# A three-block network in split fp32 on one core: the wide products of a block in a row, tiles 32 bytes further on, and another end of the convolution

## The chip, the cores and the metric

The program runs on one core of a Trainium2 chip. The metric is the device time of one execution in microseconds (us); smaller is better. What is given of the kernel before is the median of three runs, and the profile of one more execution.

## The reference

Three blocks of two layers work one after the other on `x` of 256 tokens by 1024 features in fp32. Almost all the work is dense products with weights that are each used once. The parts that matter here, cut:

```python
def swiglu_ffn(x, w_in, w_out):
    gate, up = jnp.split(x @ w_in, 2, axis=-1)
    return (jax.nn.silu(gate) * up) @ w_out

def conformer_conv_module(x, w_in, b_in, w_dw, b_dw, ln_g, ln_b, w_out, b_out):
    a, gate = jnp.split(x @ w_in + b_in, 2, axis=-1)
    h = a * jax.nn.sigmoid(gate)
    h = lax.conv_general_dilated(h, w_dw[:, None, :], ..., feature_group_count=D_MODEL) + b_dw
    h = jax.nn.silu(layer_norm(h, ln_g, ln_b))
    return h @ w_out + b_out

def reference(x, ...):
    x = first_block(x, ...)     # ffn, conv, ffn; ffn, hgrn, ffn
    x = second_block(x, ...)    # ffn, dsa attention, ffn; ffn, diff attention, ffn
    return third_block(x, ...)  # pool, mlp; moba attention, mlp
```

A feed-forward layer ("ffn") has 22 groups of 128 hidden features; the two of the third block ("mlp") have 4096 hidden features and a squared relu. The convolution is causal, 31 taps wide, one filter for each feature.

## The kernel before

**Split products.** Each fp32 operand of a big product is held as a rounded part and the rest, both in a format (`F32R`) that TensorE multiplies in one pass: weights as `hi` and `lo` (ScalarE rounds at L330, VectorE subtracts at L334), activations as `xh`, one tile that holds for each of 8 blocks of features first the rounded part of the 256 tokens and then the rest. A product of both is made of three: rounded by rounded, rounded by rest, rest by rounded. Weights come through in 413 chunks of 1 MB.

**Three forms of product.** `proj_pair` (L603 to L605) keeps an activation part of 128 tokens in the array (stationary) and streams 512 columns of weights (moving). `downs` (L644) does the same for the second product of a layer, with the hidden activations as the stationary operand: `hh` and `hl` in the feed-forward layers, `oscT` and `ov` in hgrn, `xh` itself in the other mixers. `wide_products` is turned round: it keeps 128 columns of weights in the array and streams activations. For each of the 8 blocks of features it issues a **wide** product (L565: `hi` against 512 columns, that is both parts of `xh`) and a **narrow** one (L566: `lo` against the 256 columns of the rounded part), and both add into one accumulator tile, `ps` or `tr`. Such a set of 8 wide and 8 narrow products is called a block here. Wide and narrow alternate, but for the last pair, which is the other way round.

**Layers.** A feed-forward layer begins with `first` (four weight chunks by `proj_pair`), goes on with pairs of blocks (one in `ps`, one in `tr`) and 24 or 48 products of `downs` behind each second pair, and ends in `finish`, which does `downs` for four held chunks, first for tokens 0 to 127 (accumulators `a0`, `a1`), then for the others (`a2`, `a3`). Under the second half it normalizes the first, and its transposes for the next layer (L502) are issued ten products before the end.

**The convolution.** Features stand on partitions, in 8 blocks of 128. Blocks 3 to 7 are convolved on TensorE (L930, fp32): ScalarE copies the gated block into two phases, `ph` (L928, four copies for a block), then 16 taps are multiplied for each half of the block, and ScalarE brings each half back with its bias (L934, two copies for a half). Then layer norm: VectorE subtracts a mean (L951), TensorE sums squares (L959) and the last block's mean (`rest`, L961), a reciprocal root goes over VectorE and GpSimd, TensorE spreads it over the partitions (`rb`, L973), and for two blocks at a time VectorE subtracts and multiplies (L978, L979), ScalarE applies silu and rounds (L983, L985), VectorE takes the rest (L986). The accumulators of the output projection begin with a product that puts the bias in (L990). In `ps`, `a0` to `a3` and `tr` are the PSUM tiles' names, with one buffer for each `a` and two for `ps` and `tr`: `var` is in `a3` and `ps`, `rest` in `a0`, `rb` in `a1`.

**What sets the order.** The code is recorded through a tile framework whose scheduler sets the order on each engine by the tiles' dependences, with a few fixed points (`issue`). Tiles lie in pools, one behind the other in each partition of SBUF, every tile rounded up to 32 bytes. `raw`, `hi`, `lo` and `xh` come first; then the pool of small tiles, `tiny`, with the 4-byte tile `prime`; then the pools that each layer opens and closes. In the built program `hi`, `lo` and `xh` begin 32 bytes behind a multiple of 64 (`xh` at byte 136416), and the layers' pools begin at byte 174784, a multiple of 64; `hh`, `hl`, `mh`, `ml`, `oscT` and `ov`, which lie in them, begin at multiples of 64. (`mh` and `ml` are the split memory tokens of the third block.)

The lines that the prediction speaks of, by operation: L330 and L334 splits; L502, L711 transposes; L552 to L554 `proj_u`, a run of narrow products (256 columns) in conv and hgrn; L1076 the conversion of hgrn's masks from 32 bits to 8.

Of the kernel before, what the change touches and what calls it, by code (L numbers as in the profile page):

```python
# [11 lines left out]
F32 = mybir.dt.float32  # L12
# [4 lines left out]
AF = mybir.ActivationFunctionType  # L17
OP = mybir.AluOpType
# [3 lines left out]
S = 256  # L22
# [270 lines left out]
class _K:  # L293
# [137 lines left out]
    def prime(self, func, after):  # L431

        n = after.shape[0]
        t = self.tiny.tile([128, 1], F32, name="prime", bufs=1)
        self.nc.scalar.activation(t[:n], after, func, scale=0.0)

    def square(self, src, st, n):
# [118 lines left out]
    def wide_products(self, w, p):  # L556


        wh, wl = w
        mm = self.nc.tensor.matmul  # L560
        for b, o in enumerate(p):
            for k in range(8):
                c = slice(256 * k + 128 * b, 256 * k + 128 * b + 128)
                x = self.both[:, k]
                hi = lambda start, stop: mm(o, lhsT=wh[:, c], rhs=x.rearrange("p i t -> p (i t)"), start=start, stop=stop)  # L565
                lo = lambda: mm(o[:, :256], lhsT=wl[:, c], rhs=x[:, 0], start=False, stop=False)  # L566
                if k < 7:
                    yield hi(k == 0, False)
                    yield lo()
                else:  # L570
                    yield lo()
                    yield hi(False, True)

    def added(self, out, p, n=slice(0, 128)):
        self.nc.scalar.activation(out, p[n, 256:], AF.Copy)  # L575
# [293 lines left out]
    def conv(self, act):  # L869
        nc, tc = self.nc, self.tc  # L870
        with tc.tile_pool(name="cv", bufs=2) as cp:
# [4 lines left out]
            y = cp.tile([128, 8, S], F32, name="y", bufs=1)  # L876
# [6 lines left out]
            brow = self.tmp.tile([128, D], F32, name="xn", bufs=1)  # L883
            i = _ROW[("conv_b_out", (0,))]
# [5 lines left out]
            ones = cp.tile([128, 128], F32R, name="ones", bufs=1)  # L890
            nc.scalar.activation(ones, pick[:, :128], AF.Copy)
            bias = cp.tile([128, D], F32R, name="bias", bufs=1)
            nc.scalar.activation(bias, brow, AF.Copy)
            nc.vector.tensor_tensor(bias[32:33], brow[32:33], bias[32:33].bitcast(F32), op=OP.subtract)
            self.rows_ahead("conv")

            mean = self.ps("a2")
# [6 lines left out]
            def summed(j):  # L904
                nc.tensor.matmul(mean[:, :S], lhsT=means[:, 1], rhs=y[:, j], start=(j == DVE_BLOCKS), stop=(j == DVE_BLOCKS - 1))
# [11 lines left out]
            for j in range(DVE_BLOCKS, 8):  # L917
                p = self.turned(p4[j]) if j < 4 else self.proj_u(self.take(("U", "conv", j)), act)
                g = cp.tile([128, S], F32, name="gl")
                sg = gated(j, p, g)  # L920
                x = ph[j % 2]
                pc = self.ps(f"a{j % 2}").rearrange("p (g t) -> p g t", g=4)
                for i in range(2):
                    w = cp.tile([128, 16, 128], F32, name="taps", bufs=3)
                    nc.sync.dma_start(w.rearrange("p d c -> p (d c)"), self.a["ctaps"][2 * (j - DVE_BLOCKS) + i])
                    gv = g[64 * i:64 * i + 64].rearrange("p (t a) -> p a t", a=2)
                    for a in range(2):
                        nc.scalar.activation(x[64 * a:64 * a + 64, i, 15:], gv[:, a], AF.Copy)  # L928
                    for d in range(16):
                        nc.tensor.matmul(pc[:, i], lhsT=w[:, d], rhs=x[:, i, d:d + S // 2], start=(d == 0), stop=(d == 15))  # L930
                    yv = y[64 * i:64 * i + 64, j].rearrange("p (t a) -> p a t", a=2)
                    for a in range(2):
                        h = slice(64 * a, 64 * a + 64)
                        nc.scalar.activation(yv[:, a], pc[h, i], AF.Identity, bias=self.col("bph", 2 * j + i)[h])  # L934
                if j < 7:
                    summed(j)
                self.split_ahead(2)
                n = self.TAPS_BEHIND[j - DVE_BLOCKS]
                for at in left[:n]:
                    tap(*at)  # L940
                    if at[1] == CW - 1:
                        summed(at[0])
                left = left[n:]
            self.prime(AF.Silu, sg[:, :1])

            var = [self.ps("a3"), self.ps()]
            rest = self.ps("a0")
            for b in ((0, 1), (2, 3), (4, 5), (6,), (7,)):
                n = len(b)
                yb = y[:, b[0]:b[0] + n]  # L950
# [1 line left out]
                sq = cp.tile([128, 2, S], F32, name="sq")  # L952
# [4 lines left out]
                for i in range(n):  # L957
                    for m in range(2):
                        nc.tensor.matmul(var[m][:, :1], lhsT=sq[:, i, 128 * m:128 * m + 128], rhs=means[:, 0, :1],  # L959
                                         start=(b[i] == 0), stop=(b[i] == 7))  # L960
            nc.tensor.matmul(rest[:, :S], lhsT=means[:, 0], rhs=y[:, 7], start=True, stop=True)  # L961
            t = lambda nm: self.tiny.tile([128, 2], F32, name=nm, bufs=1)
# [4 lines left out]
            nc.gpsimd.tensor_tensor(r, v, self.mhalf[:, :2], op=OP.pow)  # L967

            dg = cp.tile([128, 2, 128], F32, name="sg")
            rb = self.ps("a1")  # L970
            for m in range(2):
                nc.vector.tensor_scalar(dg[:, m], self.ident, r[:, m:m + 1], float(D), op0=OP.mult, op1=OP.mult)
                nc.tensor.matmul(rb[:, 128 * m:128 * m + 128], lhsT=means[:, 0], rhs=dg[:, m], start=True, stop=True)  # L973
            oact = self.new_act()
            for g in range(4):
                yg = y[:, 2 * g:2 * g + 2]
                for b in range(2):
                    nc.vector.tensor_tensor(yg[:, b], yg[:, b], rest[:, :S], op=OP.subtract)  # L978
                nc.vector.tensor_tensor(yg, yg, rb[:, None, :S].to_broadcast([128, 2, S]), op=OP.mult)  # L979
                z = cp.tile([128, 2, S], F32, name="sq")  # L980
                for b in range(2):
                    j = 2 * g + b
                    nc.scalar.activation(z[:, b], yg[:, b], AF.Silu, bias=self.col("lnb", j), scale=self.col("lng", j))  # L983
                h = oact[0][:, 2 * g:2 * g + 2]
                nc.scalar.activation(h, z, AF.Copy)  # L985
                nc.vector.tensor_tensor(oact[1][:, 2 * g:2 * g + 2], z, h.bitcast(F32), op=OP.subtract)  # L986
            acc = self.new_acc()
            for m in range(2):
                for n in range(2):
# [5 lines left out]
    def hgrn(self, act):  # L995
        nc, tc = self.nc, self.tc
        with tc.tile_pool(name="hg", bufs=2) as ho, ExitStack() as es:
            hp = es.enter_context(tc.tile_pool(name="hgi", bufs=2))
            masks = hp.tile([128, 7, 64], U8, name="masks", bufs=1)
# [73 lines left out]
            p4 = self.first("hgrn", _U_ORDER["hgrn"][:2], act)  # L1073
            mi = self.tmp.tile([128, D], I32, name="xn", bufs=1)
            nc.sync.dma_start(mi[:, :448], self.a["k_masks"])
            nc.vector.tensor_copy(masks.rearrange("p l t -> p (l t)"), mi[:, :448])  # L1076
            self.rows_ahead("hgrn")
            for j in range(4):
                pf, pq = ([self.turned(p4[2 * j + i]) for i in range(2)] if j < 2 else
                          [self.proj_u(self.take(("U", "hgrn", 2 * j + i)), act) for i in range(2)])  # L1080
                vals = elems(j, pf, pq)
                for lev in range(8):
                    scores(j, *vals, lev)
            for n, s in enumerate(self.HALVES):
# [8 lines left out]
            for m in range(2):  # L1093
                for h in range(8):
                    o = oacc[m][h // 4][:, 128 * (h % 4):128 * (h % 4) + 128]
# [15 lines left out]
            oact = [ho.tile([128, 8, 256], F32R, name="o" + t, tag=t, bufs=1) for t in ("v", "scT")]  # L1111
# [750 lines left out]
```

## Time and profile before

| what | value |
|---|---|
| median of three runs | 2610.27 us (2608.87 to 2611.88) |
| the profiled execution | 2617.61 us, of which its span from first to last instruction is 2615.1 us |
| TensorE | 2570.5 us busy, 98% of the span, 13302 products |
| VectorE, ScalarE | 1953.7 us (75%), 1504.6 us (58%) |
| TensorE's granted clock | 0.995 of full speed, as a mean |

"Busy" is the union of the recorded durations. TensorE's products overlap, so its busy time does not say how fast they follow each other; for that one reads the distance from one start to the next in the timeline. The profiled execution took 7.3 us longer than the median of the others.

### The profile page before, as it was taken

How to read it: one execution, taken by the hardware profiler on the slowest of the kernel's cores; microseconds unless marked ns; L12 is line 12 of the kernel's file. 1: busy time of each engine (PE TensorE's matmuls, PEld its weight loads, DVE VectorE, ACT ScalarE, POOL GpSimd, SP SyncE). 2: the span in 40 equal slices, each digit the busy share in tenths (PEclk: the TensorE clock that was granted, in tenths of full speed). 3: DMA queues.
4: the chain of work that ended last, by engine and by line, in shares of the span. 5: the costliest groups of instructions: out<-in, count | busy, mean ns of one | idle time of the engine just before them, and what ended most of it. 6: DMA issues, size and time to landing. Idle time of an engine off the chain costs nothing.

```text
span 2615.1 us, 37057 instructions
## 1 busy us (share of the span) xinstructions
PE 2570.5 (98%) x13302; PEld 2153.1 (82%) x13302; DVE 1953.7 (75%) x4175; ACT 1504.6 (58%) x3373; POOL 72.4 (3%) x158
## 2 busy tenths in 40 slices
PE   8999999999999999999999999999999999999999
PEld 7888888888888888888778888877788788877887
DVE  7868587687668886886969779777866866677664
ACT  5655455555644555655765565575655655566553
POOL 0000000000000000000000000000100000000000
PEclk9999899999999999999999999999999999999999
DMA  8847376486424675684448668653555545542552
GB/s 326 304 164 282 145 274 233 159 333 228 176 82 178 256 291 188 259 330 181 177 153 324 241 235 330 232 212 129 209 187 184 188 161 199 187 171 97 193 182 92
DMA packets 92711, 554.14 MB, mean 212 GB/s; under 512 B 10716, under 2 KB 11756, under 8 KB 38384
## 3 DMA queue, kind: packets, MB, share of 16 engines
q1 hardware_dynamic: 92528, 551.79, 57.3%
q8 instruction: 104, 1.70, 0.3%
q14 instruction: 79, 0.65, 0.1%
HBM read 550.62 MB, written 1.13 MB: 211 GB/s over the span
## 4 chain that ended last, share of the span: by engine, by line
PE 57%; issue 35%; ACT 3%; DVE 3%; DMA 1%; POOL 1%; SPq 0%; POOLq 0%; ACTq 0%; DVEq 0%
PE a L644 20%; PE ps L565 8%; PE tr L565 8%; PE ps L566 4%; PE tr L566 4%; PE a L603 2%; PE a L604 2%; PE a L605 2%; PE a L930 2%; DVE lo L334 1%; ACT hi L330 1%; PE tr L502 1%; DMA raw<-in_wall 1%; ACT junk L440 1%; POOL ry L446 1%
## 5 line engine op out<-in xcount | busy, mean ns | idle before, releaser
L334 DVE TENSOR_TENSOR lo<-raw,hi 128x512 fp32r<-128x512 f32 x1652 | 1062.5, 683 | 157.9 <-ACT hi L330 154.1
L330 ACT ACTIVATE hi<-raw 128x512 fp32r<-128x512 f32 x1652 | 926.9, 622 | 319.9 <-PE a L644 156.6
L565 PE MATMUL ps<-xh,hi 128*128 128x512 f32 x1344 | 489.1, 398 | 1.2 <-DVE sg L576 1.2
L565 PE MATMUL tr<-xh,hi 128*128 128x512 f32 x1312 | 477.5, 398 | 1.2 <-DVE ml L511 1.2
L566 PE MATMUL ps<-xh,lo 128*128 128x256 f32 x1344 | 349.9, 281 | 0.3 <-DVE lo L334 0.3
L566 PE MATMUL tr<-xh,lo 128*128 128x256 f32 x1312 | 341.9, 281 | 0.0
L644 PE MATMUL a<-hi,hh 128*128 128x512 f32 x960 | 309.5, 396 | 0.0
L644 PE MATMUL a<-hi,hl 128*128 128x512 f32 x960 | 309.3, 396 | 0.0
L644 PE MATMUL a<-lo,hh 128*128 128x512 f32 x960 | 308.9, 395 | 0.0
L565 PEld LDWEIGHTS ps<-xh,hi 128*128 128x128 f32 x1344 | 252.7, 188 | 51.3 <-DVE sg L576 1.9
L565 PEld LDWEIGHTS tr<-xh,hi 128*128 128x128 f32 x1312 | 247.7, 189 | 45.2 <-DVE ml L511 1.5
L566 PEld LDWEIGHTS ps<-xh,lo 128*128 128x128 f32 x1344 | 253.9, 189 | 15.9 <-DVE lo L334 0.5
L566 PEld LDWEIGHTS tr<-xh,lo 128*128 128x128 f32 x1312 | 248.1, 189 | 15.0
L644 PEld LDWEIGHTS a<-hi,hl 128*128 128x128 f32 x960 | 180.1, 188 | 43.4
L644 PEld LDWEIGHTS a<-lo,hh 128*128 128x128 f32 x960 | 180.1, 188 | 43.0
L644 PEld LDWEIGHTS a<-hi,hh 128*128 128x128 f32 x960 | 179.8, 188 | 40.1 <-ACT sg L832 0.2
L603 PE MATMUL a<-hi,xh 128*128 128x512 f32 x512 | 202.2, 396 | 3.1 <-ACT xh L510 1.9
L605 PE MATMUL a<-hi,xh 128*128 128x512 f32 x512 | 201.7, 395 | 0.0
L604 PE MATMUL a<-lo,xh 128*128 128x512 f32 x512 | 200.5, 392 | 0.2 <-DVE lo L334 0.2
L1186 DVE SCALAR_TENSOR_TENSOR adaj<-adaw,cond 128x1024 bf16<-128x1024 f32 x144 | 175.3, 1217 | 17.3 <-DMA adaw<-in_ada 17.0
L576 DVE TENSOR_TENSOR h<-h,tr 128x256 f32<-128x256 f32 x140 | 58.6, 419 | 150.7 <-ACT h L575 149.9
L575 ACT ACTIVATE h<-tr 128x256 f32<-128x256 f32 x140 | 53.6, 383 | 156.7 <-PE tr L565 156.6
(380 smaller groups left out, 3310.4 us busy)
## 6 DMA issues: line engine op xcount, KB each, us to landing
raw<-in_wall SPq DMA_DIRECT2D x413, 1024.0 KB, 4.8
adaw<-in_ada SPq DMA_DIRECT2D x144, 512.0 KB, 6.6
taps<-in_ctaps SPq DMA_DIRECT2D x10, 1024.0 KB, 7.4
G<-in_rows SPq DMA_DIRECT2D x16, 512.0 KB, 4.4
pg<-in_rows SPq DMA_DIRECT2D x12, 512.0 KB, 4.8
xn<-modd SPq DMA_DIRECT2D x12, 512.0 KB, 5.3
cond<-condd SPq DMA_DIRECT2D x7, 512.0 KB, 5.2
memt<-in_mem SPq DMA_DIRECT2D x4, 512.0 KB, 3.3
```

Source lines behind the costliest of these rows:

```text
L330: self.nc.scalar.activation(h[:, c], r[:, c], AF.Copy)
L334: self.nc.vector.tensor_tensor(l[:, c], r[:, c], h[:, c].bitcast(F32), op=OP.subtract)
L565: hi = lambda start, stop: mm(o, lhsT=wh[:, c], rhs=x.rearrange("p i t -> p (i t)"), start=start, stop=stop)
L566: lo = lambda: mm(o[:, :256], lhsT=wl[:, c], rhs=x[:, 0], start=False, stop=False)
L575: self.nc.scalar.activation(out, p[n, 256:], AF.Copy)
L576: self.nc.vector.tensor_tensor(out, out, p[n, :256], op=OP.add)
L603: yield self.nc.tensor.matmul(p, lhsT=xh[:, k, t], rhs=wh[:, c], start=(k == 0), stop=False)
L604: yield self.nc.tensor.matmul(p, lhsT=xh[:, k, t], rhs=wl[:, c], start=False, stop=False)
L605: yield self.nc.tensor.matmul(p, lhsT=xl[:, k, t], rhs=wh[:, c], start=False, stop=(k == 7))
L644: mm = lambda l, r, i, st, sp: nc.tensor.matmul(acc[i], lhsT=l[:k, t], rhs=r[:k, 1024 * b + 512 * i:1024 * b + 512 * i + 512], start=st, s ...
L930: nc.tensor.matmul(pc[:, i], lhsT=w[:, d], rhs=x[:, i, d:d + S // 2], start=(d == 0), stop=(d == 15))
L1186: self.nc.vector.scalar_tensor_tensor(junk, self.ada_w.pop(n), 1.0, self.cond, op0=OP.mult, op1=OP.mult, accum_out=self.mods[k][:, c:c + 1])
```

## The change

It has six parts. (1) `prime` takes 64 bytes in place of 4, of which it still uses 4; all that lies behind it, the layers' pools too, begins 32 bytes later (they at byte 174816, 32 behind a multiple of 64). (2) In a block of `wide_products` seven wide products come in a row, then the eight narrow ones, then the last wide one. (3) In the convolution's last block VectorE makes one of two copies into `ph` for each half, and one of the two copies back for the second half. (4) The layer norm's PSUM tiles move from `a0`, `a1`, `a3` to `ps` and `tr`. (5) The layer norm's end goes block by block and not two at a time. (6) The conversions of the output bias and of hgrn's masks are written later in the code.

```diff
-        t = self.tiny.tile([128, 1], F32, name="prime", bufs=1)
+        t = self.tiny.tile([128, 16], F32, name="prime", bufs=1)[:, :1]
...
         for b, o in enumerate(p):
+            c = lambda k: slice(256 * k + 128 * b, 256 * k + 128 * b + 128)
+            hi = lambda k: mm(o, lhsT=wh[:, c(k)], rhs=self.both[:, k].rearrange("p i t -> p (i t)"), start=(k == 0), stop=(k == 7))
+            for k in range(7):
+                yield hi(k)
             for k in range(8):
...
-                if k < 7:
-                    yield hi(k == 0, False)
-                    yield lo()
-                else:
-                    yield lo()
-                    yield hi(False, True)
+                yield mm(o[:, :256], lhsT=wl[:, c(k)], rhs=self.both[:, k, 0], start=False, stop=False)
+            yield hi(7)
...
-            nc.scalar.activation(bias, brow, AF.Copy)
-            nc.vector.tensor_tensor(bias[32:33], brow[32:33], bias[32:33].bitcast(F32), op=OP.subtract)
...
-                        nc.scalar.activation(x[64 * a:64 * a + 64, i, 15:], gv[:, a], AF.Copy)
+                        if j == 7 and a == 1:
+                            nc.vector.tensor_copy(x[64 * a:64 * a + 64, i, 15:], gv[:, a])
+                        else:
+                            nc.scalar.activation(x[64 * a:64 * a + 64, i, 15:], gv[:, a], AF.Copy)
...
+                        if j == 7 and i == a == 1:
+                            nc.vector.tensor_scalar(yv[:, a], pc[h, i], bd, None, op0=OP.add)
+                        else:
+                            nc.scalar.activation(yv[:, a], pc[h, i], AF.Identity, bias=bd)
                 if j < 7:
                     summed(j)
+                if j == 4:
+                    nc.scalar.activation(bias, brow, AF.Copy)
...
-            var = [self.ps("a3"), self.ps()]
-            rest = self.ps("a0")
+            var = [self.ps(), self.ps()]
+            rest = self.ps("tr")
...
-            rb = self.ps("a1")
+            rb = self.ps("tr")
...
+            for j in range(8):
+                nc.vector.tensor_tensor(y[:, j], y[:, j], rest[:, :S], op=OP.subtract)
+                nc.vector.tensor_tensor(y[:, j], y[:, j], rb[:, :S], op=OP.mult)
+                z = cp.tile([128, S], F32, name="gl")
+                nc.scalar.activation(z, y[:, j], AF.Silu, bias=self.col("lnb", j), scale=self.col("lng", j))
+                h = oact[0][:, j]
                 nc.scalar.activation(h, z, AF.Copy)
-                nc.vector.tensor_tensor(oact[1][:, 2 * g:2 * g + 2], z, h.bitcast(F32), op=OP.subtract)
+                nc.vector.tensor_tensor(oact[1][:, j], z, h.bitcast(F32), op=OP.subtract)
...
-            nc.vector.tensor_copy(masks.rearrange("p l t -> p (l t)"), mi[:, :448])
...
+                if j == 0:
+                    nc.vector.tensor_copy(masks.rearrange("p l t -> p (l t)"), mi[:, :448])
```

What the scheduler makes of it is seen in the order of the built programs (line numbers of the changed kernel differ a little). On TensorE, in a feed-forward layer, from the end of a block in `ps` into the next one in `tr`, before:

```order
L566 MATMUL ps<-xh,lo 128x256
L565 MATMUL ps<-xh,hi 128x512
L566 MATMUL ps<-xh,lo 128x256 x2
L565 MATMUL ps<-xh,hi 128x512
L565 MATMUL tr<-xh,hi 128x512
L566 MATMUL tr<-xh,lo 128x256
L565 MATMUL tr<-xh,hi 128x512
L566 MATMUL tr<-xh,lo 128x256
```

and now, both blocks whole (L564 wide, L568 narrow) and the beginning of the next:

```order
L564 MATMUL ps<-xh,hi 128x512 x7
L568 MATMUL ps<-xh,lo 128x256 x8
L564 MATMUL ps<-xh,hi 128x512
L564 MATMUL tr<-xh,hi 128x512 x7
L568 MATMUL tr<-xh,lo 128x256 x8
L564 MATMUL tr<-xh,hi 128x512
```

Eight wide products now follow each other over the border of two blocks, and eight narrow ones. On TensorE at the end of the convolution, where `y` and `sq` are the layer norm's operands and the numbers tell `a0` (2914, 2930), `a1` (2915, 2931), `a2` (2916, 2932) and `a3` (2917, 2933) of the output projection, before:

```order
L956 MATMUL a_2834<-means,y 128x1 x2
L961 MATMUL a_2834<-y,means 128x256
L959 MATMUL a_2832<-means,sq 128x1
L959 MATMUL ps<-means,sq 128x1
L990 MATMUL a_2916<-bias,ones 128x512
L990 MATMUL a_2917<-bias,ones 128x512
L973 MATMUL a_2877<-sg,means 128x128 x2
L644 MATMUL a_2916<-hi,xh 128x512
```

and now:

```order
L991 MATMUL a_2933<-bias,ones 128x512
L928 MATMUL a_2767<-ph_1952,taps 128x128 x16
L964 MATMUL ps<-means,sq 128x1 x8
L928 MATMUL a_2767<-ph_1952,taps 128x128 x16
L964 MATMUL ps<-means,sq 128x1 x6
L991 MATMUL a_2931<-bias,ones 128x512
L961 MATMUL tr<-means,y 128x1 x2
L966 MATMUL tr<-y,means 128x256
L964 MATMUL ps<-means,sq 128x1 x2
L991 MATMUL a_2932<-bias,ones 128x512
L978 MATMUL tr<-sg,means 128x128 x2
L641 MATMUL a_2930<-hi,xh 128x512
```

Two of the four bias products have moved ahead of the last block's taps (the other two stand between the sums), and the output projection now begins with `a0`, the first tokens, where it began with `a2`, the second. On VectorE around hgrn's mask conversion (`masks`), before:

```order
L511 TENSOR_TENSOR xh<-tr,xh 128x4x128 x2
L1076 CAST masks<-xn 128x448
L334 TENSOR_TENSOR lo<-raw,hi 128x512 x13
L1031 TENSOR_SCALAR T<-T,oml,lb 128x256 x2
L1033 TENSOR_TENSOR q<-X,tr 128x512
```

and now:

```order
L512 TENSOR_TENSOR xh<-tr,xh 128x4x128 x2
L1083 CAST masks<-xn 128x448
L334 TENSOR_TENSOR lo<-raw,hi 128x512 x13
L1032 TENSOR_SCALAR T<-T,oml,lb 128x256 x2
L1034 TENSOR_TENSOR q<-X,tr 128x512
```

Nothing moved there: the scheduler puts the conversion where it stood. The same holds for the two instructions of the bias.

## Rows read from the trace of the kernel before

**Rows 1.** The page: each engine's busy time, share of the span, instructions.

```profile
PE 2570.5 (98%) x13302; PEld 2153.1 (82%) x13302; DVE 1953.7 (75%) x4175; ACT 1504.6 (58%) x3373; POOL 72.4 (3%) x158
```

**Rows 2.** TensorE's waits: for whom; us in total, times, longest.

```profile
PE tr L502 <- DVE xn L487: 10.3, 3, 7.3
...
PE a L644 <- ACT xh L985: 2.6, 1, 2.6
```

**Rows 3.** TensorE's groups by line and shape: count, busy us, mean ns, idle before.

```profile
L565 PE MATMUL ps<-xh,hi 128*128 128x512 f32 x1344 | 489.1, 398 | 1.2 <-DVE sg L576 1.2
L565 PE MATMUL tr<-xh,hi 128*128 128x512 f32 x1312 | 477.5, 398 | 1.2 <-DVE ml L511 1.2
...
L644 PE MATMUL a<-hi,hh 128*128 128x512 f32 x960 | 309.5, 396 | 0.0
```

**Rows 4.** Timeline, end of the first layer, stationary hh or hl: start, us, instruction.

```profile
189.76 0.63 PE L644 MATMUL a<-hi,hh 128*128 128x512 f32 x2
...
197.70 0.63 PE L644 MATMUL a<-hi,hl 128*128 128x512 f32 x2
```

**Rows 5.** Timeline, hgrn's output projection, stationary ov or oscT.

```profile
853.62 0.62 PE L644 MATMUL a<-hi,ov 128*128 128x512 f32 x2
...
858.75 0.63 PE L644 MATMUL a<-hi,oscT 128*128 128x512 f32 x2
```

**Rows 6.** Timeline, stationary xh: last mlp's beginning, then the end of conv.

```profile
2429.52 0.39 PE L603 MATMUL a<-hi,xh 128*128 128x512 f32 x1
...
2435.86 0.39 PE L604 MATMUL a<-lo,xh 128*128 128x512 f32 x1
...
332.47 0.39 PE L644 MATMUL a<-lo,xh 128*128 128x512 f32 x1
...
334.31 0.39 PE L603 MATMUL a<-hi,xh 128*128 128x512 f32 x1
```

**Rows 7.** Timeline, from one block of wide products to the next but one.

```profile
113.60 0.40 PE L565 MATMUL ps<-xh,hi 128*128 128x512 f32 x1
113.83 0.40 PE L565 MATMUL tr<-xh,hi 128*128 128x512 f32 x1
114.07 0.28 PE L566 MATMUL tr<-xh,lo 128*128 128x256 f32 x1
...
116.66 0.40 PE L565 MATMUL ps<-xh,hi 128*128 128x512 f32 x1
```

**Rows 8.** Timeline, conv's run of narrow products.

```profile
252.05 0.28 PE L552 MATMUL ps<-xh,hi 128*128 128x256 f32 x1
...
254.81 0.28 PE L554 MATMUL ps<-xh,lo 128*128 128x256 f32 x1
```

**Rows 9.** Timeline, end of the convolution, all engines; in brackets the idle time before.

```profile
287.48 1.32 ACT L928 ACTIVATE ph<-gl 64x128 f32<-64x128 f32 x4
288.18 5.47 PE L930 MATMUL a<-ph,taps 128*128 128x128 f32 x32 [2.25 <-ACT ph L928]
...
299.04 0.75 ACT L934 ACTIVATE y<-a,cols 64x128 f32<-64x128 f32 x2 [3.21 <-PE a L930]
...
301.96 0.41 DVE L978 TENSOR_TENSOR y<-y,a 128x256 f32<-128x256 f32 x1
...
304.52 0.69 DVE L979 TENSOR_TENSOR y<-y,a 128x512 f32<-128x512 f32 x1 [0.52 <-PE a L973]
...
305.24 1.09 ACT L983 ACTIVATE sq<-y,cols 128x256 f32<-128x256 f32 x2 [3.52 <-DVE y L979]
...
312.76 0.57 PE L990 MATMUL a<-bias,ones 128*128 128x512 f32 x1
...
330.85 1.32 PE L502 MATMUL tr<-ident,xn 128*128 128x128 f32 x8 [0.71 <-DVE xn L487]
```

**Rows 10.** Windows: us, busy by engine, PEclk (granted clock), DMA share, GB/s.

```profile
304.00:316.00 12.00, 9.43 (x30) 7.31 (x29) 6.90 (x13) 6.87 (x13) 0.00 (x0) 0.62 0.08 24
```

**Rows 11.** Timeline, hgrn's mask conversion on VectorE; in brackets the idle time before.

```profile
728.64 0.39 DVE L1076 CAST masks<-xn 128x448 uint8<-128x448 int32 x1 [6.40 <-DMA xn<-in_k_masks]
```

More of the change, by code (lines that the diff above doesn't have):

```diff
@@ L561, in wide_products @@
         for b, o in enumerate(p):
+            c = lambda k: slice(256 * k + 128 * b, 256 * k + 128 * b + 128)
+            hi = lambda k: mm(o, lhsT=wh[:, c(k)], rhs=self.both[:, k].rearrange("p i t -> p (i t)"), start=(k == 0), stop=(k == 7))
+            for k in range(7):
+                yield hi(k)
             for k in range(8):
[L563 to L566, printed above, removed]
-                if k < 7:
-                    yield hi(k == 0, False)
-                    yield lo()
-                else:
-                    yield lo()
-                    yield hi(False, True)
+                yield mm(o[:, :256], lhsT=wl[:, c(k)], rhs=self.both[:, k, 0], start=False, stop=False)
+            yield hi(7)
     def added(self, out, p, n=slice(0, 128)):
@@ L933, in conv @@
                         h = slice(64 * a, 64 * a + 64)
-                        nc.scalar.activation(yv[:, a], pc[h, i], AF.Identity, bias=self.col("bph", 2 * j + i)[h])
+                        bd = self.col("bph", 2 * j + i)[h]
+                        if j == 7 and i == a == 1:
+                            nc.vector.tensor_scalar(yv[:, a], pc[h, i], bd, None, op0=OP.add)
+                        else:
+                            nc.scalar.activation(yv[:, a], pc[h, i], AF.Identity, bias=bd)
                 if j < 7:
                     summed(j)
+                if j == 4:
+                    nc.scalar.activation(bias, brow, AF.Copy)
+                    nc.vector.tensor_tensor(bias[32:33], brow[32:33], bias[32:33].bitcast(F32), op=OP.subtract)
                 self.split_ahead(2)
@@ L974, in conv @@
             oact = self.new_act()
[L975 to L984, printed above, removed]
+            for j in range(8):
[4 more added lines that the diff above has]
+                h = oact[0][:, j]
                 nc.scalar.activation(h, z, AF.Copy)
-                nc.vector.tensor_tensor(oact[1][:, 2 * g:2 * g + 2], z, h.bitcast(F32), op=OP.subtract)
+                nc.vector.tensor_tensor(oact[1][:, j], z, h.bitcast(F32), op=OP.subtract)
             acc = self.new_acc()
```

## The prediction, made before the changed kernel ran

> **What bounds the kernel now.** I read the page first, for the engine that is never free. TensorE is busy 98% of the span, VectorE 75%, ScalarE 58% [rows 1]. Next come TensorE's waits: two of the larger ones are 10.3 us for the transposes that turn a layer's result and 2.6 us in the convolution [rows 2]. So most of the 2615.1 us span is products that follow each other, and a change of the order or of the operands counts only through the distance from one product's start to the next. No view prints that distance, and the recorded durations hide it: a product of 512 columns is recorded with 0.39 to 0.40 us in every group [rows 3], while in the timeline the next one starts after some 0.23. So I took starts from the timeline, over long unbroken runs, and divided by the number of products between them.
>
> Three paces come out for the same 128x512 product, with the clock at its upper level in each of these stretches.
> - Stationary `hh` or `hl`: from 189.76 to 197.70 there are 17 rows of two, 34 products; 7.94 / 34 = 233.5 ns [rows 4].
> - Stationary `ov` or `oscT`: from 853.62 to 858.75, 22 products; 5.13 / 22 = 233.2 ns [rows 5].
> - Stationary `xh`: from 2429.52 to 2435.86, 28 products, 6.34 / 28 = 226.4 ns; in the first eight after a break, from 332.47 to 334.31, 1.84 / 8 = 230 ns [rows 6].
>
> What tells the third case from the first two is the tile that is loaded into the array. `xh` begins 32 bytes behind a multiple of 64; the others begin on one. The moving operand is `hi` or `lo` in all of them.
>
> A block of wide products takes 116.66 - 113.83 = 2.83 us for 16 products [rows 7]. Inside it wide to narrow takes 114.07 - 113.83 = 0.24, and wide to wide, at the border, 113.83 - 113.60 = 0.23. A long run of narrow ones goes at (254.81 - 252.05) / 23 = 120 ns [rows 8].
>
> **The change, term by term.**
>
> *1. The 32 bytes.* They bring `hh`, `hl`, `oscT` and `ov` to where `xh` stands, 32 behind a multiple of 64. If the offset makes the pace, they take on the pace of `xh`. There are 3 x 960 = 2880 such products in feed-forward layers: the group of [rows 3] counts 960 for `hi` by `hh`, and the two cross products are as many. A settled run would save 233.5 - 226.4 = 7.1 ns for each, the first ones after a break 233.5 - 230 = 3.5. A run of `downs` is 24 or 48 products and is broken by blocks and transposes, so I count half of them as settled: 1440 x 7.1 + 1440 x 3.5 = 10.2 + 5.0 = **15.3 us less**. Bounds: nothing, if the place in SBUF and not the offset makes the difference (every slow tile lies behind byte 174784, every fast one ahead of it), and 2880 x 7.1 = 20.4. `ov`, `oscT` and the split memory tokens move too; they are few and stay out of the sum.
>
> *2. The order in a block.* Same products, same sums; what changes is who follows whom. The two wide, two narrow pattern leaves one wide-to-narrow and one narrow-to-wide change where it had eight or so. The trace has no run of wide products with weights as stationary. Bounds from the nearest rows: at the settled pace of `xh` runs 8 x 226.4 + 8 x 120 = 2.771 us, 0.049 less than the 2.82 that a block takes as a mean of several; at the pace of the border step, 235 (0.23 to 0.24 in the rows), 8 x 235 + 8 x 120 = 2.84, 0.02 more. (1344 + 1312) / 8 = 332 blocks [rows 3], so the term lies between -16.3 and +6.6 us. I take the unsettled pace, because eight in a row is the length over which [rows 6] show 230: 8 x 230 + 8 x 120 = 2.80, 0.015 to 0.02 less, **5 us less**. The weights are no obstacle to seven wide products in a row: the wait before all 1344 wide products into `ps` is 1.2 us in sum, and before those into `tr` 1.2 [rows 3].
>
> The Trainium skill ("TensorE: Matmul & The Clock Gate", section "Back-to-back issue gap") gives the distance between isolated products as columns / 2.4 + 2.5 ns, about 216 for 512 columns and 109 for 256, by columns alone. The trace does not agree: it has 226.4, 230 and 233.5 for 512 and 120 for 256 [rows 4, 6, 8]. By that rule terms 1 and 2 would both be nothing; this is a rival below.
>
> *3. The convolution's end.* Here TensorE does wait, so time taken from ScalarE and VectorE count.
> - TensorE waits 2.25 us for `ph`, four copies of 1.32 us together, 0.33 each [rows 9]. With VectorE making one of two for a half, the first half's pair is there one copy sooner: -0.3.
> - The copies back of the second half, two in 0.75 [rows 9], go to two engines: -0.37.
> - Subtract and multiply before the first `silu`: 256 wide for one block in place of 512 for two, 0.41 in place of 0.69 [rows 9]: -0.27. ScalarE's next steps become half as long (two of them take 1.09 us in the pair [rows 9], but a second, smaller copy adds its fixed cost): -0.25 of what TensorE waits for `xh` (2.6 us in one wait [rows 2]).
> - The products that put the bias in: one is recorded at 312.76, in the middle of the output projection [rows 9]. In the new order they stand before the last taps and between the sums, where TensorE waits anyway. The granted clock is 0.62 of full speed there [rows 10], so they cost about 0.43 for the one and 0.23 for the other, by the pace of [rows 7] at either level: -0.66.
> - The projection now begins with the first tokens, so the next layer's transposes find their half normalized sooner; the gap of 0.71 before them [rows 9] goes: -0.7.
>
> The sum is **2.5 us less**. Bounds: nothing, if TensorE then waits for VectorE in the same places (its L978 and L979 are now 16 short instructions for 4 blocks of two, with the fixed cost of each), and -5, if the waits of 2.25 and 2.6 both go whole.
>
> *4. The later conversions.* The order on VectorE shows them where they stood. The mask conversion waits 6.40 us for its data [rows 11], and it will again. **Nothing**, because neither the instruction nor its data come at another time; if the conversion did move behind the first scores' operands, VectorE would have those 6.40 us for other work, and the splits behind it would come earlier.
>
> Sum: -15.3 - 5 - 2.5 = -22.8 us. The profiled execution takes 2617.6 and would take 2594.8; the other runs' median is 7.3 us lower, and I carry the gain over whole: 2610.3 - 22.8 = **2587.5 us**.
>
> **Rivals.**
> - *The place, not the offset.* Term 1 is nothing. For it: the slow and the fast stationary tiles also differ in where they lie. Against it: within the slow ones the pace is the same over tiles far apart (233.5 and 233.2). 2610.3 - 7.5 = 2602.8 us.
> - *Wide products in a row are slow.* The block's pattern paid for its border step only once; eight steps of 235 cost 0.02 a block, +6.6 instead of -5. For it: the one wide-to-wide step in the rows is not faster than wide to narrow. Against it: a step beside a change of accumulator need not be that of a run. 2610.3 - 15.3 + 6.6 - 2.5 = 2599.1 us.
> - *Columns alone.* The products keep their paces whatever follows and wherever the tile lies; what differs in the rows comes from the layer they stand in. Only the convolution's end is left: 2610.3 - 2.5 = 2607.8 us. Against it: the same output projection code gives both paces [rows 5, 6]. This is the case in which the skill's rule of columns decides.
> - *The other side.* The offset matters, but to the sum of both operands and not to the stationary one by itself: `hi` and `lo` too begin 32 behind a multiple of 64, and two tiles with the same offset may meet in the same place. Then `hh` runs take the slowest step of the rows, 240 ns [rows 7], in place of 233.5: 2880 x 6.5 = +18.7, less the 7.5 of the other terms: 2610.3 + 11.2 = 2621.5 us. It makes the kernel slower once `hh` runs exceed 233.5 + 7.5 / 2.88 = 236.1 ns. Against it: `xh` by `hi`, both at 32, is the fastest row of all.
>
> **Chances and range.** The forecast, with offset and order both some gain, has 0.70, and its own range is 2576 to 2596: term 1 between 11 and 20, term 2 between 0 and 11. Slow wide runs have 0.10, the place 0.09, columns alone 0.06, the other side 0.05. A measurement of this kernel tells some 0.2% from no change, 5.2 us. Faster than 2605.1 are the forecast, slow wide runs and nearly all of the place: 0.86. Within 5.2 us of before lie columns alone and the slow edge of the place: 0.09. Slower: 0.05. The range for 8 in 10 reaches from 2574 to 2603; below it lie only settled paces everywhere, above it the last two rivals.
>
> **What would show it.** In the trace of the changed kernel: `downs` in a feed-forward layer near 228 ns from start to start (233.5 if the place decides, 240 on the other side); a block near 2.80 us (2.77 at best, 2.84 if wide runs are slow), with the narrow ones at 120; in the convolution a wait below 2.25 before the last taps, the bias product gone from the projection's middle, no gap before the next layer's transposes; and the mask conversion still waiting 6.4 us. I would be wrong most of all if the pace depends on a thing that I have not separated from the offset, or if a run of wide products with weights loaded as stationary has a pace of its own.

## The result and the profile after

The changed kernel takes 2584.79 us as the median of four runs (2581.25 to 2585.82), the kernel before 2611.07 (three of its four runs are those given above): a ratio of 0.9898, with a 95% interval of 0.9881 to 0.9915, or 26 us less. In a later set of runs it was 0.9880 (0.9864 to 0.9896). The forecast was 2587.5, within a range of 2574 to 2603.

The page of the changed kernel, the line of busy times and instruction counts:

```profile
span 2584.0 us, 37067 instructions
...
PE 2537.3 (98%) x13302; PEld 2147.7 (83%) x13302; DVE 1953.3 (76%) x4186; ACT 1501.2 (58%) x3374; POOL 72.2 (3%) x158
```

TensorE does the same 13302 products, is busy for the same 98% of the span, and the span is 31.1 us shorter [rows 1]; that is more than 26 because the execution of the kernel before that was profiled was a long one. So what changed is chiefly how fast products follow each other. The waits hardly moved: all that are listed for TensorE add up to 38.9 us before and 40.8 now. Two of them, for whom, in all, how often, the longest:

```profile
PE tr L503 <- DVE xn L488: 9.9, 2, 7.5
...
PE a L641 <- ACT xh L986: 1.9, 1, 1.9
```

10.3 us became 9.9, and 2.6 became 1.9 [rows 2].

The timeline at the end of the first layer, where `hh` and `hl` are the stationary operands (L641 is the old L644):

```profile
186.96 0.61 PE L641 MATMUL a<-hi,hh 128*128 128x512 f32 x2
...
194.66 0.62 PE L641 MATMUL a<-hi,hl 128*128 128x512 f32 x2
```

From the first row up to the last there are 17 rows of two, 34 products as in [rows 4]: 7.70 / 34 = 226.5 ns, where it was 233.5. The recorded duration hides nearly all of that; it went from 0.63 to 0.62.

Two blocks of wide products in the first layer (L564 wide, L568 narrow):

```profile
112.10 1.77 PE L564 MATMUL tr<-xh,hi 128*128 128x512 f32 x7
113.71 1.11 PE L568 MATMUL tr<-xh,lo 128*128 128x256 f32 x8
114.66 0.40 PE L564 MATMUL tr<-xh,hi 128*128 128x512 f32 x1
114.89 1.77 PE L564 MATMUL ps<-xh,hi 128*128 128x512 f32 x7
```

A block now takes 114.89 - 112.10 = 2.79 us, against 2.83 [rows 7]. The seven wide products take 113.71 - 112.10 = 1.61, 230 ns each, and the eight narrow ones 114.66 - 113.71 = 0.95, 119 each.

The end of the convolution on TensorE; in brackets the idle time before:

```profile
286.62 3.81 PE L928 MATMUL a<-ph,taps 128*128 128x128 f32 x32 [1.62 <-ACT ph L926]
...
291.97 3.82 PE L928 MATMUL a<-ph,taps 128*128 128x128 f32 x32
...
302.58 1.22 PE L641 MATMUL a<-hi,xh 128*128 128x512 f32 x2 [1.94 <-ACT xh L986]
...
324.88 1.03 PE L503 MATMUL tr<-ident,xn 128*128 128x128 f32 x8
```

The two rows of taps are the two halves of the last block (each of the 16 taps leaves two records). From the first half's taps to the next layer's transposes it was 330.85 - 288.18 = 42.67 us [rows 9] and is 324.88 - 286.62 = 38.26. The transposes have no idle time ahead of them. The second half's taps and the output projection began in the kernel before at

```profile
295.19 3.82 PE L930 MATMUL a<-ph,taps 128*128 128x128 f32 x32
...
307.05 1.22 PE L644 MATMUL a<-hi,xh 128*128 128x512 f32 x2 [2.57 <-ACT xh L985]
```

So three parts became shorter: from half to half 7.01 us became 5.35, from the second half to the projection 11.86 became 10.61, from there to the transposes 23.80 became 22.30. In the first part the taps that were recorded with 5.47 us [rows 9] take 3.81; the windows of the old and of the new end further down show that this is the clock. The mask conversion, on VectorE:

```profile
717.63 0.39 DVE L1083 CAST masks<-xn 128x448 uint8<-128x448 int32 x1 [6.09 <-DMA xn<-in_k_masks]
```

It waits for its data as it did [rows 11].

### The profile page after: what moved, and what is told of

Its sections match the earlier page's. It is cut to its first block, busy times and chain, and to the rows that moved or that the text cites. A ratio compares the mean times of both kernels' runs of the same rounds, so it can differ in the third digit from the quotient of the medians.

```text
span 2584.0 us, 37067 instructions
## 1 busy us (share of the span) xinstructions
PE 2537.3 (98%) x13302; PEld 2147.7 (83%) x13302; DVE 1953.3 (76%) x4186; ACT 1501.2 (58%) x3374; POOL 72.2 (3%) x158
## 4 chain that ended last, share of the span: by engine, by line
PE 57%; issue 35%; DVE 3%; ACT 3%; DMA 2%; POOL 1%; SPq 0%; POOLq 0%; ACTq 0%; DVEq 0%
PE a L641 20%; PE ps L564 8%; PE tr L564 8%; PE ps L568 4%; PE tr L568 4%; PE a L600 2%; PE a L601 2%; PE a L602 2%; PE a L928 1%; DVE lo L334 1%; ACT hi L330 1%; DMA raw<-in_wall 1%; PE tr L503 1%; POOL ry L447 1%; PE ps L601 1%
## 5 line engine op out<-in xcount | busy, mean ns | idle before, releaser
L564 PE MATMUL ps<-xh,hi 128*128 128x512 f32 x1344 | 363.2, 392 | 0.9 <-DVE sg L573 0.9
L564 PE MATMUL tr<-xh,hi 128*128 128x512 f32 x1312 | 355.3, 392 | 1.2 <-DVE ml L512 1.2
L641 PE MATMUL a<-hi,hh 128*128 128x512 f32 x960 | 305.1, 391 | 0.0
L641 PE MATMUL a<-lo,hh 128*128 128x512 f32 x960 | 304.1, 390 | 0.0
L641 PE MATMUL a<-hi,hl 128*128 128x512 f32 x960 | 303.5, 390 | 0.0
L564 PEld LDWEIGHTS ps<-xh,hi 128*128 128x128 f32 x1344 | 253.0, 189 | 45.3 <-DVE sg L573 1.2
L564 PEld LDWEIGHTS tr<-xh,hi 128*128 128x128 f32 x1312 | 247.6, 189 | 43.7 <-DVE ml L512 1.5
L641 PEld LDWEIGHTS a<-lo,hh 128*128 128x128 f32 x960 | 180.2, 188 | 38.3
L641 PEld LDWEIGHTS a<-hi,hl 128*128 128x128 f32 x960 | 180.3, 188 | 37.9
L641 PEld LDWEIGHTS a<-hi,hh 128*128 128x128 f32 x960 | 180.2, 188 | 34.6
L568 PEld LDWEIGHTS ps<-xh,lo 128*128 128x128 f32 x1344 | 183.5, 190 | 13.3 <-DVE lo L334 0.2
L568 PEld LDWEIGHTS tr<-xh,lo 128*128 128x128 f32 x1312 | 179.5, 190 | 12.8
L568 PE MATMUL ps<-xh,lo 128*128 128x256 f32 x1344 | 187.8, 282 | 0.0
L568 PE MATMUL tr<-xh,lo 128*128 128x256 f32 x1312 | 184.9, 283 | 0.0
L751 ACT ACTIVATE sg<-sg 128x256 f32<-128x256 f32 x144 | 60.2, 418 | 131.8 <-DVE sg L573 131.8
```

The lines of the kernel that those rows point to most:

```text
L564: hi = lambda k: mm(o, lhsT=wh[:, c(k)], rhs=self.both[:, k].rearrange("p i t -> p (i t)"), start=(k == 0), stop=(k == 7))
L568: yield mm(o[:, :256], lhsT=wl[:, c(k)], rhs=self.both[:, k, 0], start=False, stop=False)
L641: mm = lambda l, r, i, st, sp: nc.tensor.matmul(acc[i], lhsT=l[:k, t], rhs=r[:k, 1024 * b + 512 * i:1024 * b + 512 * i + 512], start=st, s ...
L751: nc.scalar.activation(sg[:n], sg[:n], AF.Silu)
```

## The experiments

**Each main part alone, and another shift.** The kernel before had a median of 2612.47 us in this set of runs.

*e1_offset* is the kernel before with one edit:

```diff
-        t = self.tiny.tile([128, 1], F32, name="prime", bufs=1)
+        t = self.tiny.tile([128, 16], F32, name="prime", bufs=1)[:, :1]
```

> The kernel before with the 64-byte prime tile alone. Theory (the offset of the stationary tile sets the pace): the downs products with hh and hl go from 234 ns from start to start to about 228, the time falls by 15 to 17 us, to about 2594; blocks of wide products stay at 2.82 us. Rival (the gain came from the other order around the downs): hh stays near 234, the time within 2 us of before.

Measured: 2597.43 us, ratio 0.9944 (0.9931 to 0.9958), 14.6 us less by the ratio. The first long run of `downs`, and the wide product behind it, in the timeline:

```profile
49.07 0.62 PE L644 MATMUL a<-hi,hh 128*128 128x512 f32 x2
...
59.95 0.39 PE L565 MATMUL ps<-xh,hi 128*128 128x512 f32 x1
```

48 products in 10.88 us, 226.7 ns each; the first step takes 233, every other one 226 or 227. Over all 2880 products with `hh` or `hl` the mean distance to the next start goes from 233.8 in the trace of the kernel before to 227.9 here, which makes 17 us. Nothing else was edited, so the shift alone does it, as the theory had it; which operand the offset belongs to is tested further down.

*e2_order* is the kernel before with the new `wide_products` alone:

```diff
+            for k in range(7):
+                yield hi(k)
             for k in range(8):
...
+                yield mm(o[:, :256], lhsT=wl[:, c(k)], rhs=self.both[:, k, 0], start=False, stop=False)
+            yield hi(7)
```

> The kernel before with the new order in a block alone. Theory (fewer changes between wide and narrow): a block goes from 2.82 to 2.793 us, the time falls by 9 to 10 us, to about 2601; downs stay at 234 ns. By the sum of the prediction it would be 5 us less, 2605. Rival (the order needs the offset, because the downs runs end each pair of blocks): less than 2 us.

Measured: 2602.33 us, ratio 0.9961 (0.9947 to 0.9975), 10.2 us less. Its blocks in the timeline (narrow products at L567, wide ones at L563):

```profile
114.00 1.77 PE L563 MATMUL tr<-xh,hi 128*128 128x512 f32 x7
115.60 1.11 PE L567 MATMUL tr<-xh,lo 128*128 128x256 f32 x8
116.56 0.40 PE L563 MATMUL tr<-xh,hi 128*128 128x512 f32 x1
116.79 1.77 PE L563 MATMUL ps<-xh,hi 128*128 128x512 f32 x7
```

2.79 us a block, as in the changed kernel: the order needs no help of the offset. As a mean over the 322 blocks of each trace that ran without a lower clock or a break, a block takes 2.818 us in the kernel before and 2.789 here; 0.029 x 332 = 9.6 us, which agrees with the time and with the theory.

*e3_conv* is the changed kernel with the two edits above undone, so that parts 3 to 6 of the change are left:

```diff
-        t = self.tiny.tile([128, 16], F32, name="prime", bufs=1)[:, :1]
+        t = self.tiny.tile([128, 1], F32, name="prime", bufs=1)
...
+                if k < 7:
+                    yield hi(k == 0, False)
+                    yield lo()
```

> The changed kernel without the larger prime tile and with the old order in a block: what is left is the convolution's end and the later conversions. Theory: 2.5 to 5 us less than before, 2605 to 2608; the traces of before and after show 4.7 us less from the last taps but one to the next layer's transposes. Rival (what TensorE gains there is waited for in the next layer): within 1 us of before.

Measured: 2610.39 us, ratio 0.9995 (0.9987 to 1.0004), 1.3 us less, with an interval from 3.4 less to 1.0 more. By time alone the convolution's end can't be told from nothing here, and the 2.5 to 5 us of the expectation were not reached. The rows of its trace, and behind them the transposes after the next layer in the kernel before:

```profile
287.77 3.81 PE L932 MATMUL a<-ph,taps 128*128 128x128 f32 x32 [1.63 <-ACT ph L930]
...
325.94 1.03 PE L503 MATMUL tr<-ident,xn 128*128 128x128 f32 x8
...
514.56 1.03 PE L503 MATMUL tr<-ident,xn 128*128 128x128 f32 x8
```

```profile
519.25 1.03 PE L502 MATMUL tr<-ident,xn 128*128 128x128 f32 x8
```

The stretch of 42.67 us takes 325.94 - 287.77 = 38.17 here, and the next layer does not give it back: 514.56 - 325.94 = 188.62 us, against 519.25 - 330.85 = 188.40 before. So the trace shows neither the rival nor the small gain of the runs; why the runs gained less than the trace stays open.

*e4_shift64* is the changed kernel with another size of the tile:

```diff
-        t = self.tiny.tile([128, 16], F32, name="prime", bufs=1)[:, :1]
+        t = self.tiny.tile([128, 24], F32, name="prime", bufs=1)[:, :1]
```

> The changed kernel with a prime tile of 96 bytes: the layers' pools begin 64 bytes behind their place in the kernel before, on a multiple of 64 again. Theory (offset): downs back to 234 ns, 15 to 17 us more than the changed kernel, about 2601. Rival (the place: any shift away from byte 174784 will do): downs stay at 228, time as the changed kernel, about 2585.

Measured: 2600.28 us, ratio to the kernel before 0.9956 (0.9943 to 0.9969), so the gain of the offset is gone. The run that is shown for e1_offset, here:

```profile
48.70 0.62 PE L641 MATMUL a<-hi,hh 128*128 128x512 f32 x2
...
59.90 0.62 PE L564 MATMUL ps<-xh,hi 128*128 128x512 f32 x2
```

48 products in 11.20 us, 233.3 ns. The tiles lie further from their old place than in the changed kernel, and they are slow again. The place does not count; what the three shifts (0, 32 and 64 bytes) fit is the remainder by 64.

**Whose offset.** *e5_weights0* moves the other side. `raw`, `hi`, `lo` and `xh` go to multiples of 64, and `hh`, `hl`, `oscT`, `ov` stay 32 behind one:

```diff
+        self.pad = pool("pad", 1).tile([128, 8], F32, name="pad")
         self.raw_p = pool("rawp", self.RB)
...
-        t = self.tiny.tile([128, 16], F32, name="prime", bufs=1)[:, :1]
+        t = self.tiny.tile([128, 1], F32, name="prime", bufs=1)
```

> The changed kernel with 32 bytes put ahead of the raw weights and the old 4-byte prime tile: raw, hi, lo and xh now begin on multiples of 64, hh, hl, oscT, ov stay 32 behind one. Theory (the stationary tile's offset alone): downs stay at 228 ns; runs with xh as stationary go from 227 to 233 ns and blocks get longer, by some 2640 x 6.5 and 2656 x 5 ns, so 30 us more than the changed kernel, about 2615. Rival (stationary and moving must have the same offset): downs go to 234 ns, xh runs and blocks stay, 15 to 17 us more, about 2601. A third outcome (the moving tile's offset counts for itself) would show in both.

Measured: 2601.50 us, ratio 0.9949 (0.9933 to 0.9965; the kernel before had 2613.99 in this set). The same run of `downs`, and then one with `xh` as the stationary operand, in the last layer:

```profile
49.17 0.62 PE L642 MATMUL a<-hi,hh 128*128 128x512 f32 x2
...
60.36 0.62 PE L565 MATMUL ps<-xh,hi 128*128 128x512 f32 x2
...
2414.25 0.39 PE L601 MATMUL a<-hi,xh 128*128 128x512 f32 x1
...
2422.63 0.39 PE L602 MATMUL a<-lo,xh 128*128 128x512 f32 x1
```

`downs` takes 11.19 / 48 = 233.1 ns, though `hh` stands where it was fast. `xh` takes 8.38 / 37 = 226.5 ns, though it now begins on a multiple of 64. The blocks, with both operands at 0, stay at 2.79 as a mean. So it is not the stationary tile's own offset. Both operands at 32 are fast (the changed kernel), both at 0 are fast (`xh` by `hi` here), one at each is slow (the kernel before and this one, with the roles changed). The pace goes by whether the two agree. The rival that was named in the expectation holds, and my theory falls.

**Longer rows.** *e6_sixteen* puts the two blocks of a chunk together:

```diff
+        for b in range(len(p)):
+            for k in range(7):
+                yield hi(b, k)
+        for b, o in enumerate(p):
+            for k in range(8):
+                yield mm(o[:, :256], lhsT=wl[:, c(b, k)], rhs=self.both[:, k, 0], start=False, stop=False)
+        for b in range(len(p)):
+            yield hi(b, 7)
```

> The changed kernel with the two blocks of a chunk put together: seven wide products of each, then sixteen narrow ones, then the two last wide ones, so 16 wide and 16 narrow follow each other. Theory (each change from narrow to wide costs some 25 ns, and half of them go): 0.02 us for each of 166 pairs, 3 us less, about 2582. Rival (the first tile of a pair is ready a block later, and ScalarE and VectorE then hand over the hidden features too late): waits before downs, 2585 or more.

Measured: 2592.42 us, ratio 0.9915 (0.9899 to 0.9931), less than the changed kernel gains in its two sets (0.9898 and 0.9880). A pair of blocks in its timeline, then a place in the second layer, and the row of waits that sums such places up:

```profile
115.11 1.76 PE L563 MATMUL ps<-xh,hi 128*128 128x512 f32 x7
116.71 1.75 PE L563 MATMUL tr<-xh,hi 128*128 128x512 f32 x7
118.30 1.12 PE L569 MATMUL ps<-xh,lo 128*128 128x256 f32 x8
...
120.68 0.62 PE L643 MATMUL a<-hi,hh 128*128 128x512 f32 x2
...
357.91 0.73 PE L563 MATMUL tr<-xh,hi 128*128 128x512 f32 x2 [1.71 <-DVE hl L719]
```

```profile
PE tr L563 <- DVE hl L719: 7.5, 6, 1.8
```

The pair takes 120.68 - 115.11 = 5.57 us where two blocks took 2 x 2.79 = 5.58; the first seven wide products take 1.60, the next seven 1.59. As a mean over 125 pairs of each trace it is 5.561 us against 5.576 in the changed kernel, so some 15 ns a pair are gained, 2.6 us over 166 pairs. The waits cost more, though not where the rival had them, ahead of `downs`. Six times a wide product waits for the split of the transposed features, which are issued in the middle of the first pair and hold the `tr` buffer.

*e7_sixteen_later* leaves that first pair in the order of the changed kernel, and ran beside the changed kernel (*e9_after*) and a kernel with offset and order but the old convolution (*e8_offset_order*, the edits of e1_offset and e2_order together). In this set the kernel before had 2616.17 us.

```diff
-                    products = self.wide_products(w, p)
+                    products = self.wide_products(w, p, f > 4)
```

> As the kernel with 16 wide and 16 narrow products in a row, but the first pair of blocks of each feed-forward layer, under which the transposes are issued, keeps the order of the changed kernel. Theory (only that pair made the waits of the sixteen): the waits of wide products for hl go, the gain of some 20 ns for each later pair stays, 2 to 3 us less than the changed kernel (run in the same set). Rival (a pair that is ready later costs in every pair): 2 us or more above the changed kernel.

> The kernel before with the larger prime tile and the new order in a block, with the old end of the convolution: offset and order together, 24 to 25 us less than before if the two add (15.0 and 10.1 apart), 1 to 4 us more than the changed kernel of the same set. Rival (the convolution's new end brings nothing that lasts): equal to the changed kernel within 1 us.

> The changed kernel again, as the measure for the other two of this set: 26 to 27 us less than before.

Measured: e7 2582.79 us, 0.9874 (0.9860 to 0.9889); e8 2587.97 us, 0.9891 (0.9877 to 0.9906); e9 2583.74 us, 0.9880 (0.9864 to 0.9896). Of the waits for `hl` one is left in e7's list:

```profile
PE tr L563 <- DVE hl L720: 1.0, 1, 1.0
```

The 1 us between e7 and e9 is within what the intervals leave open, so e7 is no proven improvement. e8 is 28.5 us below the kernel before by its ratio; the single gains of 14.6 and 10.2 add within their intervals. e9 is 31.4 us below by its ratio, more than I expected. Between e8 and e9 lie 4.2 us by the medians, with overlapping intervals. How far a run moves with the clock is seen in the four of e9: 2577.55 and 2580.84 us at a mean granted clock of 0.999 and 0.998, 2586.63 and 2587.63 at 0.996. That is more than the convolution's end is worth, so the time of few runs can't settle it.

**The clock in the convolution.** The old end, in the kernel with offset and order (e8), then the new one in the changed kernel; windows from the taps of the last block's first half to those of its second half, which the expectations below call the last taps but one and the last block's taps (us, busy by engine, the granted clock PEclk, DMA share, GB/s):

```profile
287.20:294.40 7.20, 7.11 (x49) 7.11 (x50) 2.99 (x6) 5.21 (x11) 0.00 (x0) 0.76 0.41 146
```

```profile
286.60:292.00 5.40, 5.38 (x49) 5.40 (x49) 3.59 (x7) 4.69 (x9) 0.00 (x0) 1.00 0.34 127
```

The same taps and sums take some 1.7 us longer in the old end, at a granted clock of 0.76 in place of 1.00. To see which edit does it, one copy was taken out and put in by itself. *e10_ph_scalar* is the changed kernel with all copies into `ph` on ScalarE; *e11_ph_only* is the kernel before with the shared copies alone.

```diff
-                        if j == 7 and a == 1:
-                            nc.vector.tensor_copy(x[64 * a:64 * a + 64, i, 15:], gv[:, a])
-                        else:
-                            nc.scalar.activation(x[64 * a:64 * a + 64, i, 15:], gv[:, a], AF.Copy)
+                        nc.scalar.activation(x[64 * a:64 * a + 64, i, 15:], gv[:, a], AF.Copy)
```

> The changed kernel with all four copies into the last block's phases on ScalarE again. Theory (the shorter wait ahead of the last taps but one keeps the clock up): TensorE waits some 2.2 us there and the taps and sums behind it, to the last block's taps, take 7.0 us at a granted clock below 1 in place of 5.35. Rival (the clock falls there for another reason, such as the PSUM tiles): the wait grows, the stretch stays at 5.35. The time itself moves by less than one run can tell.

> The kernel before with only the copies into the last block's phases shared with VectorE. Theory: the wait ahead of the taps falls from 2.25 to about 1.6 us and the stretch to the last block's taps from 7.0 to 5.35 us, the clock at 1.00. Rival: the wait falls and the stretch stays at 7.0.

Measured, in one run each: 2586.26 us for e10 and 2616.49 for e11, beside 2616.46 for the kernel before. The rows of e10, then of e11:

```profile
283.62 0.40 PE L988 MATMUL a<-bias,ones 128*128 128x512 f32 x1
285.80 3.84 PE L925 MATMUL a<-ph,taps 128*128 128x128 f32 x32 [1.79 <-ACT ph L923]
...
291.18 3.82 PE L925 MATMUL a<-ph,taps 128*128 128x128 f32 x32
```

```profile
291.34 5.44 PE L933 MATMUL a<-ph,taps 128*128 128x128 f32 x32 [2.24 <-DVE ph L929]
```

Both expectations fail. With every copy on ScalarE the wait grows by 0.17 us only, and the stretch stays short, 291.18 - 285.80 = 5.38. With the shared copies alone the wait stays at 2.24, now for VectorE's copies, and the 32 records take 5.44 us, where they take 3.84 in e10. What shortens the idle time is the two bias products that now stand in it: 2.25 - 1.79 = 0.46 us, about two products of 0.23. They can stand there because part 4 took the layer norm's tiles out of `a0` and `a3`. In all eight traces with them ahead of the taps (the changed kernel's, e3 to e7, e9, e10) the stretch took 5.4 us; of the five without them (before, e1, e2, e8, e11) four took 6.9 to 7.0 and one, e2, took 5.4. So the clock goes with their place in the traces. That they are the cause is argued and not shown: no run moved them alone, and the eight traces have the other parts of the new end as well. Since e2 kept its clock behind the longer wait, the wait does not decide every time.

## Why the prediction was right

*The bound.* Right: TensorE stayed at 98%. The single gains of the two edits that touch only the pace of products (e1 and e2) add up to 24.8 us of the 26, and the two together (e8) gave 28.5 of the 31.4 in their set.

*Term 1, the offset, 15.3 us less.* The size was right: 14.6 by e1_offset (11 to 18 by its interval). The reason was half right. I gave `hh` the pace of `xh` because the stationary tile would stand where `xh` stands; e5_weights0 shows that it is fast because it agrees with the moving operand, and that the same 32 bytes make it slow when the weights are moved. The rows of the kernel before could not tell the two apart, since there the moving operand was always at 32. That the size came out all the same is no accident, because with the moving operand at 32 both reasons give the same paces; for a kernel with its weights elsewhere mine would have been wrong, as e5_weights0 shows. The half that I counted as unsettled at 230 is not in the rows: e1_offset's first run is at 226 or 227 from its second step on. What keeps the term below 2880 x 7.1 = 20.4 us is the mean: over all products the trace has 233.8 - 227.9 = 5.9 ns, 17 us, and the measured 14.6 has that within its interval.

*Term 2, the order, 5 us less.* Right in sign, half the size: 10.2 by e2_order (6.5 to 13.8). The pace of wide products in a row was well chosen, 230 ns in the rows of the changed kernel. The step that was off is the difference. By the means of the traces a block went from 2.818 to 2.789; my 8 x 230 + 8 x 120 = 2.800 was 0.011 too long, chiefly because narrow ones in a row of eight go at 119 and not 120 (0.95 / 8), and I then took 0.015 where 2.818 - 2.800 is 0.018. Together that is 0.014, and 0.014 x 332 is the missing 5 us. With a few hundredths of a microsecond times 332, the third digit is what counts.

*Term 3, the convolution, 2.5 us less.* By time not told from nothing: 1.3 less by e3_conv (3.4 less to 1.0 more), 4.2 by the medians of e8 and e9. In the trace the stretch named above is 4.4 us shorter, and 1.66 of that, from half to half, I had not seen at all: it is the clock, which fell there in four of five traces of the old end and in none of the new one. Without it the stretch is 2.75 shorter, near the forecast. From the second half to the projection it is 1.25, where I had 0.89 for the copies back, the first block and ScalarE's steps; of this the wait before the projection, 2.6 [rows 2] and now 1.9, is a part. From there to the transposes it is 1.50, where I had 0.66 for the bias products and 0.7 for the gap, which is gone as forecast. (The 0.43 for a bias product at the lower clock level, 1.2 GHz, is not in [rows 7]; the products ahead of the one at 312.76 do follow each other at 426 to 428 ns.) The shared copies shortened the wait ahead of the taps by 0.17 us (1.79 in e10, 1.62 in the changed kernel) and not by 0.3. The single edits behind the taps did not run by themselves.

*Term 4, nothing.* Right as far as the order and the wait of 6.09 us show; it did not run by itself.

*The sum.* The measured single gains are 14.6 + 10.2 + 1.3 = 26.1 us, where I had 22.8. That the forecast is only 2.7 us off is in part luck: term 2 was 5 too small, terms 1 and 3 by these times 2 too large.

*The rivals.* The place falls by e4_shift64. Slow wide products in a row fall by e2_order. Columns alone, and with it the Trainium skill's rule as the prediction had it, falls by e1_offset and e2_order: neither changes a product's columns, and the time falls by 14.6 and 10.2. The Trainium skill ("TensorE: Matmul & The Clock Gate", section "Back-to-back issue gap") has columns / 2.4 + 2.5 ns for isolated products, 216 for 512; no stretch here comes below 226. The other side, that two tiles at the same offset get in each other's way, is the reverse of what e5_weights0 shows.

## What to carry to other kernels

Where a kernel is bound by products one after the other, measure the distance between starts over long runs, by pairs of tiles: the recorded durations and busy shares hid 3% here. If two kinds of runs differ, look up where their tiles begin, and try the same remainder by 64 bytes for both operands of a product, as it paid here for `F32R`; a few unused bytes ahead of a pool can do it. Then let products of one size follow each other. Small independent products in TensorE's idle time ahead of a dense stretch are worth a trial: here the clock went with them, without proof that they kept it.

## What was not expected of the hardware

The pace of a 128x512 product in `F32R` depends on two tiles together: 226.5 to 226.7 ns when they begin at the same remainder by 64 bytes (both 32 or both 0), 233 to 233.5 when they don't. All four combinations ran, both at 0 with `xh` as the stationary operand only, and all tiles lie on multiples of 32, so no other remainder was tried. Why is not settled by these runs.

Behind narrow products the wide ones need some steps until they are at their pace. In the changed kernel's trace the seven of a block take 1.61 us behind another block, whose end is eight narrow ones and one wide one (mean of 168), and 1.59 behind a run of `downs`, which is all of 512 columns (mean of 68). In e6_sixteen the seven that follow a first seven take 1.59 too.

A difference of 0.46 us in the idle time of TensorE (2.25 against 1.79) went with a stretch of taps that took 1.7 us longer, at a granted clock of 0.76, in four of five traces against none of eight.
